# The transfers of the forget-bias rows are issued from the SP queue instead of ScalarE's

## The chip, the cores and the metric

The kernel runs on one core of a Trainium2 chip. The metric is the device time of one execution in microseconds. The core has TensorE (PE in the profile; its weight loads are PEld), VectorE (DVE), ScalarE (ACT), GpSimd (POOL) and SyncE (SP). SP does no arithmetic here: its queue issues transfers. ScalarE has a queue from which it can issue transfers too, between its own instructions.

## The reference

The program computes two layers of a decoder trunk for one sequence of 512 positions and 1024 features in float32. A layer normalises the residual, projects it to queries, keys, values and gates of sixteen heads of 64 features, runs two kinds of attention, gates and projects the result, adds it to the residual, and adds a gated embedding. Eight heads are dilated (three windows mixed) and eight are forgetting heads. For a forgetting head the logit of query i and key k has the difference of two running sums of log forget gates added:

```python
c = jnp.cumsum(log_f.astype(jnp.float32), axis=1).transpose(0, 2, 1)
s = jnp.einsum('bqhd,bkhd->bhqk', q_i, k, preferred_element_type=jnp.float32) * scale
s = s + c_i[..., :, None] - c[:, :, None, :]
```

The part that depends on the query alone drops out of the softmax, so the kernel adds only the row of the key, one row of 512 numbers for each head.

## The kernel before

Float32 products are made on TensorE from pairs: each matrix is split into a high part and a remainder, and a product is three matmuls (`mm3`, over line 88). The weights come from memory by SP (`load`, line 115) into one of three raw buffers, and are split by ScalarE (line 157, `whi`) and VectorE (line 158, `wlo`); the raw buffer is then free for the third load after it. Calls of `W.pump` in the program place these splits among the other work.

In each layer a loop runs over `p`, the eight pairs of heads: pairs 0 to 3 are dilated, 4 to 7 are forgetting. An iteration projects pair `p` for four blocks of 128 positions (`pj`, evacuated by `ev`: squares on ScalarE at line 440, values at line 451, a power on GpSimd at line 445), makes scores and softmax of pair `p-1` (`att_s`: lines 597 to 601), multiplies the probabilities of pair `p-2` with the values (`att_pv`), computes the gate of pair `p` (`gate_mm`, then line 482 on VectorE and line 483 on ScalarE), transposes the probabilities (`att_tp`, evacuated by `att_pt` at lines 621 and 622) and the queries and keys (`att_z`, evacuated by `att_qk` at lines 548 to 556). All matmuls stand on TensorE in the order of the program text. The order on the other engines and in the queues is drawn up ahead of time by a planner, from the text, the dependencies and estimated costs; an engine and a queue then execute their own list strictly in order, each item waiting for what it needs.

At `p == 4` the running sums are made (`cumulate`): a high part by ScalarE into `C2[0:8]` (line 513) and a remainder by VectorE into `C2[32:40]` (line 514). `bias_rows(p)` then copies, for the two heads of pair `p`, one row of high parts and one of remainders from `C2` into four partitions of `CB`: four transfers of 2 KB. It is called at `p` = 4, 5, 6 and 7 of both layers, so there are 8 groups and 32 transfers. They are issued from ScalarE's queue (line 523). A group needs `C2`, and its target `CB` must have been read by the scores of the pair before. It is read by the scores of its own pair one iteration later: the matmuls `psS<-CB,tri` and `psM<-CB,tri` in `att_s`, with 64 rows of `CB` for a head, of which all but two are zero.

Of the kernel before, what the change touches and what calls it, by code (L numbers as in the profile page):

```python
# [9 lines left out]
F32 = mybir.dt.float32  # L10
# [191 lines left out]
def trunk(tc, ap):  # L202
    nc = tc.nc
    V, A, G, T = nc.vector, nc.scalar, nc.gpsimd, InOrder(tc, nc.tensor)
    ctx = ExitStack()
    with ctx:
# [63 lines left out]
        CB = cp.tile([P, S], F32R, name="CB")  # L270
# [247 lines left out]
        def bias_rows(a):  # L518

            for j in range(2):  # L520
                h = 2 * (a - NDIL) + j
                for i in range(2):
                    A.dma_start(CB[64 * j + i:64 * j + i + 1].bitcast(F32),  # L523
                                C2[32 * i + h:32 * i + h + 1].bitcast(F32))


# [157 lines left out]
        for l in range(DEPTH):  # L684
# [58 lines left out]
            for p in range(1, NPAIR):  # L743
# [30 lines left out]
                if NDIL <= p < NPAIR and a >= NDIL:  # L774
                    bias_rows(p)
                pj(p, 3)
                ev(p, 3)
                if p == NDIL:
                    cumulate()
                    bias_rows(p)  # L780
# [186 lines left out]
```

## Time and profile before

| what | value |
|---|---|
| median of the runs | 712.31 us |
| the profiled execution, device time | 712.22 us |
| its span (first to last instruction) | 710.4 us |
| TensorE busy with matmuls | 699.4 us (98%) |
| TensorE loading weights | 618.4 us (87%) |
| VectorE busy | 501.8 us (71%) |
| ScalarE busy | 382.3 us (54%) |
| GpSimd busy | 182.9 us (26%) |
| mean granted TensorE clock | 0.999 |

Busy times leave out what a queue does: the issue of a transfer by ScalarE is in no busy time, but shows as a row of ACTq, ScalarE's queue. So ScalarE can be held up while it counts as idle. The 1.8 us between the span and the device time lie around the first and the last instruction.

### The profile page before, as it was taken

The numbers are of one execution on the slowest core, as the hardware profiler recorded it, in microseconds if no ns is written. First come the engines' busy times: TensorE is split into PE (matmuls) and PEld (weight loads), VectorE is DVE, ScalarE is ACT, GpSimd is POOL, SyncE is SP. The second block draws the span as 40 slices with busy tenths as digits, with TensorE's granted clock in tenths as the row PEclk, the third lists the DMA queues.
The fourth block names the chain that finished last, engine by engine and source line by source line (L and its number), as shares of the span: only waits on it lengthen the run. The fifth ranks groups of instructions, "written<-read, shape, count | busy, mean of one in ns | idle before, by whom it ended". The sixth has DMA issues, their size and how long they took to land.

```text
span 710.4 us, 12211 instructions
## 1 busy us (share of the span) xinstructions
PE 699.4 (98%) x4424; PEld 618.4 (87%) x4424; DVE 501.8 (71%) x1240; ACT 382.3 (54%) x809; POOL 182.9 (26%) x326
## 2 busy tenths in 40 slices
PE   9999999999999999999999999999999999999997
PEld 8999898989989878888899899998889897888886
DVE  7887787766767677838738687777767767694633
ACT  8575556555555756525425556555654656582310
POOL 7462643313131320000004533614131240200000
PEclk9999999999999999999999999999999999999999
DMA  8612131221212145424423022222222113353211
GB/s 289 194 32 68 57 99 50 86 68 54 90 57 88 36 139 150 157 83 156 139 69 119 8 90 60 84 67 70 73 65 86 60 61 119 105 163 118 89 44 45
DMA packets 23948, 65.53 MB, mean 92 GB/s; under 512 B 4817, under 2 KB 6097, under 8 KB 23889
## 3 DMA queue, kind: packets, MB, share of 16 engines
q1 hardware_dynamic: 22576, 64.68, 28.6%
q8 instruction: 35, 0.57, 0.3%
q10 hardware_dynamic: 1312, 0.08, 0.1%
q14 instruction: 25, 0.20, 0.1%
HBM read 60.49 MB, written 4.19 MB: 91 GB/s over the span
## 4 chain that ended last, share of the span: by engine, by line
PE 64%; DVE 17%; ACT 8%; issue 4%; POOL 4%; ACTq 2%; DMA 0%; POOLq 0%; DVEq 0%
PE psA L88 42%; PE psS L88 16%; DVE wlo L158 5%; PE psM L88 4%; POOL f L445 3%; DVE PT L622 3%; ACT U L599 3%; ACTq L523 2%; ACT PT L621 1%; DVE U L597 1%; DVE U L653 1%; ACT whi L157 1%; ACT sqh L483 1%; DVE V L452 1%; DVE ms L442 1%
## 5 line engine op out<-in xcount | busy, mean ns | idle before, releaser
L157 ACT ACTIVATE whi<-raw 128x1024 fp32r<-128x1024 f32 (+3 forms) x105 | 106.7, 1021 | 68.2 <-PE psA L88 51.7
L158 DVE TENSOR_TENSOR wlo<-raw,whi 128x1024 fp32r<-128x1024 f32 (+3 forms) x105 | 122.8, 1171 | 13.3 <-ACT whi L157 13.2
L88 PE MATMUL psA<-whi,X 128*128 128x384 f32 (+1 forms) x480 | 130.5, 341 | 0.0
L88 PE MATMUL psA<-whi,Y 128*128 128x384 f32 (+1 forms) x480 | 129.3, 341 | 0.2 <-DVE U L482 0.2
L445 POOL TENSOR_TENSOR f<-ms,mhalf 128x4 f32<-128x4 f32 x64 | 64.7, 1012 | 243.7 <-DVE ms L443 234.1
L88 PE MATMUL psA<-Y,whi 128*128 128x512 f32 (+1 forms) x320 | 96.6, 385 | 0.7 <-DVE sqh L863 0.5
L88 PE MATMUL psA<-X,whi 128*128 128x512 f32 x304 | 95.7, 396 | 0.0
L599 ACT ACTIVATE U<-U,mx 128x512 f32<-128x512 f32 (+3 forms) x128 | 70.6, 553 | 39.4 <-DVE mx L597 34.5
L88 PEld LDWEIGHTS psA<-whi,X 128*128 128x128 f32 x480 | 87.9, 188 | 1.8 <-ACT whi L157 0.5
L88 PEld LDWEIGHTS psA<-whi,Y 128*128 128x128 f32 x480 | 87.5, 188 | 1.4 <-issue 0.4
L88 PE MATMUL psA<-wlo,X 128*128 128x384 f32 (+1 forms) x240 | 81.8, 341 | 1.7 <-DVE wlo L158 1.7
L88 PE MATMUL psA<-wlo,Y 128*128 128x384 f32 (+1 forms) x240 | 81.3, 339 | 1.2 <-DVE wlo L158 1.2
L601 POOL TENSOR_SCALAR U<-U,sm 128x512 f32<-128x512 f32 (+3 forms) x128 | 65.8, 534 | 55.0 <-DVE sm L600 54.2
L88 PEld LDWEIGHTS psA<-Y,whi 128*128 128x128 f32 x320 | 58.4, 188 | 13.5 <-DVE sqh L863 1.2
L88 PEld LDWEIGHTS psA<-X,whi 128*128 128x128 f32 x304 | 56.5, 188 | 13.1 <-DVE sqh L863 0.4
L88 PE MATMUL psA<-Y,wlo 128*128 128x512 f32 (+1 forms) x160 | 61.3, 383 | 0.0
L88 PE MATMUL psA<-X,wlo 128*128 128x512 f32 x152 | 59.9, 394 | 0.0
L458 DVE TENSOR_TENSOR z<-psA,f 128x256 f32<-128x256 f32 x60 | 25.4, 423 | 45.9 <-POOL f L445 45.9
L622 DVE TENSOR_TENSOR PT<-psS,PT 128x512 fp32r<-128x512 f32 (+1 forms) x58 | 37.1, 673 | 19.1 <-ACT PT L621 19.1
L440 ACT ACTIVATE sq<-psA 128x256 f32<-128x256 f32 x56 | 21.3, 381 | 53.4 <-PE psA L88 45.8
L88 PEld LDWEIGHTS psA<-wlo,X 128*128 128x128 f32 x240 | 45.2, 188 | 3.2 <-DVE wlo L158 3.2
L88 PEld LDWEIGHTS psA<-wlo,Y 128*128 128x128 f32 x240 | 45.1, 188 | 2.0 <-DVE wlo L158 2.0
(190 smaller groups left out, 1232.5 us busy)
## 6 DMA issues: line engine op xcount, KB each, us to landing
raw<-in_wq_dram SPq DMA_DIRECT2D x28, 576.0 KB, 3.9
raw<-in_wg_dram SPq DMA_DIRECT2D x16, 512.0 KB, 3.4
raw<-in_wo_dram SPq DMA_DIRECT2D x16, 512.0 KB, 3.4
raw<-in_wpg_dram SPq DMA_DIRECT2D x16, 512.0 KB, 3.4
raw<-in_wq_dram SPq DMA_DIRECT2D x14, 384.0 KB, 3.3
U<-in_xT_dram SPq DMA_DIRECT2D x16, 256.0 KB, 3.9
raw<-in_wple_dram SPq DMA_DIRECT2D x4, 512.0 KB, 3.6
hs<-U SPq DMA_DIRECT2D x8, 256.0 KB, 3.2
```

Of the source, the lines that this page charges most:

```text
L88: return self.tc.keep_in_program_order(self.eng.matmul(*a, **k))
L157: self.nc.scalar.activation(hi, r, AF.Copy)
L158: eng.tensor_tensor(lo, r, hi.bitcast(F32), op=ALU.subtract)
L440: A.activation(sq, ps[:, :2 * P].rearrange("p (h d) -> p h d", h=4), AF.Square)
L442: V.tensor_reduce(ms, sq, axis=AX.X, op=ALU.add)
L445: G.tensor_tensor(f, ms, mhalf.to_broadcast([P, 4]), op=ALU.pow)
L452: V.scalar_tensor_tensor(v2[:, t, :, HD:P], vps, st["r"][:, t:t + 1], v2[:, t, :, 0:HD].bitcast(F32), op0=ALU.mult, op1=ALU.subtract)
L458: last["V"] = V.tensor_tensor(z, ps[:, :2 * P].rearrange("p (h d) -> p h d", h=4), f[:, :, None].to_broadcast([P, 4, HD]), op=ALU.mult)
L523: A.dma_start(CB[64 * j + i:64 * j + i + 1].bitcast(F32), C2[32 * i + h:32 * i + h + 1].bitcast(F32))
L599: A.activation(seg, seg, AF.Exp, bias=mx, scale=-1.0, accum_out=sm)
L601: G.tensor_scalar(seg, seg, sm, 1.0, op0=ALU.mult, op1=ALU.mult)
L622: last["V"] = V.tensor_tensor(lo, src, hi.bitcast(F32), op=ALU.subtract)
```

## The change

The four transfers of `bias_rows` are issued through `nc.sync`, the SP queue, on which the loads of the weights and the reads and writes of the residual stand. Source, target, size, number, and place in the program text stay as they are.

```diff
@@ -520,7 +520,7 @@
             for j in range(2):
                 h = 2 * (a - NDIL) + j
                 for i in range(2):
-                    A.dma_start(CB[64 * j + i:64 * j + i + 1].bitcast(F32),
+                    nc.sync.dma_start(CB[64 * j + i:64 * j + i + 1].bitcast(F32),
                                 C2[32 * i + h:32 * i + h + 1].bitcast(F32))
```

## Rows read from the trace of the kernel before

**Rows 1.** The page, section 1: busy time, share of the span, instructions.
```profile
PE 699.4 (98%) x4424; PEld 618.4 (87%) x4424; DVE 501.8 (71%) x1240; ACT 382.3 (54%) x809; POOL 182.9 (26%) x326
```
**Rows 2.** Busy time in three stretches: limits, length, then PE, PEld, DVE, ACT, POOL, clock.
```profile
140.00:256.00 116.00, 114.22 (x817) 101.89 (x817) 83.58 (x213) 66.50 (x154) 28.75 (x46) 1.00 0.24 74
256.00:488.00 232.00, 231.82 (x1380) 204.29 (x1379) 164.57 (x388) 121.51 (x243) 53.88 (x90) 1.00 0.31 98
488.00:605.00 117.00, 115.44 (x832) 103.45 (x830) 84.92 (x220) 67.32 (x157) 29.28 (x47) 1.00 0.24 75
```
**Rows 3.** The page, section 4: shares of the chain that ended last, by engine.
```profile
PE 64%; DVE 17%; ACT 8%; issue 4%; POOL 4%; ACTq 2%; DMA 0%; POOLq 0%; DVEq 0%
```
**Rows 4.** The tile CB: its transfers (ns min/median/max, starts), and their time to landing.
```profile
L523 ACTq DMA_DIRECT2D CB<-C x32: 504/546/1271, 147.4 to 585.5; - x32
...
DMA to landing us min/median/max: 1.6/1.7/4.5
```
**Rows 5.** Timeline of ACT, first group: start, us, what [idle before, what ended it].
```profile
147.44 2.52 ACTq L523 DMA_DIRECT2D CB<-C  x4
150.01 0.63 ACT L483 ACTIVATE sqh<-U 128x512 f32<-128x512 f32 x1 [2.60 <-issue]
```
**Rows 6.** Timeline of DVE behind the first group.
```profile
148.16 0.69 DVE L482 TENSOR_TENSOR U<-psA,Rh 128x512 f32<-128x512 f32 x1
151.30 1.29 DVE L622 TENSOR_TENSOR PT<-psS,PT 128x512 fp32r<-128x512 f32 x2 [2.45 <-ACT PT L621]
...
154.00 0.95 DVE L158 TENSOR_TENSOR wlo<-raw,whi 128x768 fp32r<-128x768 f32 x1
```
**Rows 7.** Timeline of PE at the stall behind the first group, and at undisturbed pace.
```profile
154.09 0.33 PE L88 MATMUL psA<-whi,X 128*128 128x384 f32 x1
155.00 0.44 PE L88 MATMUL psA<-wlo,X 128*128 128x384 f32 x1 [0.58 <-DVE wlo L158]
...
186.22 0.51 PE L88 MATMUL psA<-whi,X 128*128 128x384 f32 x2
```
**Rows 8.** Timeline of ACT, the end of the second group and what follows.
```profile
175.13 0.60 ACTq L523 DMA_DIRECT2D CB<-C  x1
175.83 0.39 ACT L440 ACTIVATE sq<-psA 128x256 f32<-128x256 f32 x1 [0.98 <-ACT U L599]
...
180.59 0.63 ACT L483 ACTIVATE sqh<-U 128x512 f32<-128x512 f32 x1 [3.06 <-DVE U L482]
```
**Rows 9.** Timeline of DVE behind the second group.
```profile
178.61 1.35 DVE L158 TENSOR_TENSOR wlo<-raw,whi 128x1152 fp32r<-128x1152 f32 x1
179.88 0.68 DVE L482 TENSOR_TENSOR U<-psA,Rh 128x512 f32<-128x512 f32 x1
```
**Rows 10.** Waits of PE for the split of weights: us in total, times, longest.
```profile
PE psA L88 <- DVE wlo L158: 2.9, 8, 0.6
```
**Rows 11.** Timeline of PE: four more stalls, the first two with no group near.
```profile
5.88 0.70 PE L88 MATMUL psA<-wlo,X 128*128 128x392 f32 x1 [0.20 <-DVE wlo L158]
...
123.64 0.45 PE L88 MATMUL psA<-wlo,X 128*128 128x384 f32 x1 [0.37 <-DVE wlo L158]
...
185.94 0.44 PE L88 MATMUL psA<-wlo,X 128*128 128x384 f32 x1 [0.39 <-DVE wlo L158]
...
529.85 0.41 PE L88 MATMUL psA<-whi,Y 128*128 128x384 f32 x1 [0.18 <-DVE U L482]
```
**Rows 12.** Waits of the SP queue: us in total, times, longest.
```profile
SPq L115 <- DVE wlo L158: 543.0, 90, 21.8
```
**Rows 13.** Timeline of SP: two loads behind the first group.
```profile
161.48 0.33 SPq L115 DMA_DIRECT2D raw<-in_wq_dram  x1
166.52 0.33 SPq L115 DMA_DIRECT2D raw<-in_wg_dram  x1
```
**Rows 14.** Timeline of PE: the first matmuls that read the first group's rows.
```profile
166.56 0.40 PE L88 MATMUL psS<-CB,tri 64*128 64x512 f32 x2
```
**Rows 15.** The page, section 6: loads, KB each, median us from issue to landing.
```profile
raw<-in_wq_dram SPq DMA_DIRECT2D x28, 576.0 KB, 3.9
```

## The prediction

> **What bounds the kernel now.** I read the page's busy times first, then the same times by stretch, then the chain, and only then the place of the change. TensorE is busy 98% of the span [rows 1]. By stretch [rows 2] it idles 116.00 − 114.22 = 1.78 us in 140 to 256 and 117.00 − 115.44 = 1.56 us in 488 to 605, the two stretches that hold the 8 groups and what follows them, but only 0.18 us in the 232 us between, at a granted clock of 1.00 in all. So the matmuls set the time, and the change can touch TensorE's idle time alone: 3.34 us where the groups stand.
>
> The chain seems to say more: 2% of it is ACTq, ScalarE's queue [rows 3], some 14 us of 710. That is a share of one path through the other engines. TensorE worked beside it nearly all the time, and those parts of the path can shrink without moving the end.
>
> **What is removed.** ScalarE loses 32 issues of 546 ns (median; 504 to 1271) [rows 4], 17.5 us of its queue. In the first group of a layer the four stand between ScalarE's instructions: it issues from 147.44 for 2.52 us, and its next instruction, the gate's tanh, starts at 150.01 after 2.60 us of idleness that nothing but the issue explains [rows 5]. Its input was ready when VectorE ended line 482, at 148.16 + 0.69 = 148.85 [rows 6]. So the tanh, and all behind it, can come 150.01 − 148.85 = 1.16 us earlier, not 2.6. Behind it the trace runs: evacuation of the transposed probabilities on ScalarE, its remainder on VectorE at 151.30 after 2.45 us of waiting for ScalarE, and at 154.00 the split of the weights for the matmul at hand [rows 6]. For that split TensorE waits: a matmul starts at 155.00, 0.91 us after the one before it [rows 7], where two such matmuls take 0.51 us together and one 0.34, hence 0.17 apart [rows 7]. The stall costs 0.74 us: 0.58 idle and 0.16 by which the earlier one's shadow covers it. A relief of 1.16 us removes it whole.
>
> In the second group the first issues run under the exponentials and cost nothing. The last two stand out: the last is issued at 175.13, and the next instruction starts at 175.83 after 0.98 us of idleness [rows 8]. The idleness is put down to ACT itself, which had long been done, so I put it down to the issues. What follows goes squares, power on GpSimd, scaling, split of weights, and line 482 right behind that split on VectorE [rows 9]; the tanh waited 3.06 us for it [rows 8]. Each link starts as the one before it ends, so the relief of 0.98 us carries to the split for which TensorE stalls by 0.39 us [rows 11], and 0.39 + 0.16 = 0.55 is less than 0.98.
>
> **The sum.** TensorE waited 2.9 us in 8 stalls for such a split [rows 10]. Two of them have no group near, 0.20 and 0.37 [rows 11], which leaves 2.33 us in 6 stalls, behind the first three groups of each layer. One more wait of 0.18 us, for line 482, stands behind a group [rows 11]. That is 2.51 us of idleness, and with 0.16 us for each of 7 stalls, 1.12, a gain of 3.63 us. The last group of a layer stands before further small stalls: 3.34 − 2.51 = 0.83 us of the idle time is there or scattered. They hang on the values' matmuls after the loop, where ScalarE and VectorE have several evacuations in a row; I count them at nothing. With them, and 0.16 for each of about four, 1.5 us, the largest gain would be 5.1 us. The lower bound of the gain is nothing, if other waits take the stalls' place: the stall of 0.37 us at 123.64 shows that one of this kind forms with no issue on ScalarE.
>
> **What is added to SP.** 32 issues. SP's own take 0.33 us [rows 13], ScalarE's 0.55; so 1.3 to 2.2 us for a group. SP waits for splits 543 of 710 us [rows 12], so the time is there. Two waits come with it. The rows wait for `C2` and for the last reading of `CB`; the loads behind them wait too. For the first group `C2` is complete only at about 148.1, so a load listed behind it would go out up to about 4 us late. Such a load fills a buffer that is read three splits on, and splits, to judge by the loads that they let out, are 5 us apart [rows 13]: some 10 us of slack, no cost. Other loads are further from the groups. The rows in turn may wait behind loads. They land 1.7 us after their issue [rows 4], by 4 × 0.55 + 1.7 = 3.9 us as a group, some 151, and the first reading is at 166.56 [rows 14]. That slack of 15 us is the cover; the price once it is gone is a rival below. In bytes nothing changes: 2 KB each.
>
> Against the profiled execution's 712.22 us the sum gives 712.2 − 3.6 = **708.6 us**. The median of the runs is 712.31, 0.1 away, so both name the same start.
>
> **Rivals.**
>
> *The waits are only handed on.* The planner draws up ScalarE's and VectorE's lists anew without the issues, and may put the splits elsewhere; or the relief ends at VectorE, busy 72% in these stretches. For it: the stall at 123.64. Against it: each chain above is unbroken, and the relief is longer than the stalls. At no gain the time is 712.3; if each of the 8 groups got a stall like 123.64's, 0.37 + 0.16 = 0.53, in addition, 716.5.
>
> *The rows come late.* SP executes in order and stands 76% of the time waiting for a split [rows 12]. If the planner lists a group behind loads whose splits come much later, the scores wait for `CB` on TensorE, in program order with everything behind them. For the first group it takes the load at 166.52: then the rows go out from 166.85 for 1.3 us and land 1.7 us later, at 169.9, against the reading at 166.56: 3.3 us. Listed behind the load at 161.48 they land at about 164.8, in time. With eight such groups 26.6 us, and 712.2 − 3.6 + 26.6 = 735. It passes 2% (14.2 us) from six groups on: 17.8 us, which is 14.2 + 3.6. Against it: a group is ready 10 us or more before that load, and a planner that takes what is ready would not pass it over.
> A rule makes this a little worse: the Trainium skill, "DMA: Bandwidth & Descriptors", section on queues, rings and completion order, has SP and ScalarE own one ring each on the same 16 engines, worked off in ring order. A load lands after 3.9 us [rows 15]; rows right behind that at 161.48 would by the rule land only after it, at 165.4 or later, close to 166.56. No row here shows small transfers behind a load on one queue; the slack of the likeliest order, 15 us, covers 3.9.
>
> *The chain's share comes back whole.* 2% of 710 is 14 us: 698. That would need TensorE to have room at its pace. The Trainium skill, "Perfetto Trace Analysis", section on the most-contended engine, says just this, that matmul busy time is no measure of headroom and the weight loads' share is; that share is 87% here, which would leave 13% of room. The trace speaks against it for this change: PEld is busy 88% of the stretch without groups (204.29 of 232.00), 88% of the two with them (101.89 of 116.00, 103.45 of 117.00) [rows 2]. If the issues slowed TensorE beyond its idle time, the share would drop there.
>
> **How the numbers follow.** Stalls gone, 707.1 to 710: 0.62. Handed on, with no gain or with new stalls, 711 to 716.5: 0.31, most of it within 2 us of 712.3. Rows late: 0.04, half of it past 2%. The whole share: 0.02; a remainder of 0.01 for a faster one still. The predicted time is the first case's. The range reaches from 706.0, a little beyond the largest gain (707.1), to 714.5, which takes in the second case but for its end: about 0.88, and less than that since the bounds are estimates. A difference of under 2% (14 us, what a measurement of this kernel can tell from no change) has 0.95: the first case and nearly all of the second lie in it. Faster by more: 0.02, the third rival. Slower by more: 0.03, late rows in six or more groups, or a worse list.
>
> **What would show it.** Right: no L523 on ACTq; the tanh that started 2.57 us after the first issue [rows 5] starts within a few tenths of the end of line 482; the six stalls on line 158 shrink to under 1 us in all; TensorE's idle time in the two stretches falls from 3.34 to about 0.8; SP issues `CB` right after the last reading of the group before. Wrong: TensorE waiting at `psS<-CB,tri` for a DMA (late rows); loads that land after ScalarE asks for them; stalls on line 158 as long as before, at other places (handed on). A gain of over 5.1 us would say that the idle time is not the bound that I take it for.

## The result, and the profile after

The changed kernel takes 706.61 us (four runs, 706.42 to 706.83). Of the four runs of the kernel before, one took 1372.89 us and is left out here; the other three have a median of 711.92 (712.12 with it). So the change takes off 5.3 us, a ratio of 0.9925 with a 95% interval of 0.9906 to 0.9945. The forecast was 708.6 and the range 706.0 to 714.5; the sign and the mechanism were right, the size was too small. The difference is clear of the noise and under the 2% to which the prediction gave 0.95.

From the page of the changed kernel, section 1, and section 4's shares by engine, which answer to [rows 1, 3]:

```profile
PE 696.0 (99%) x4424; PEld 618.3 (88%) x4424; DVE 502.3 (71%) x1240; ACT 382.3 (54%) x809; POOL 183.5 (26%) x326
...
PE 88%; DVE 6%; ACT 3%; POOL 1%; issue 1%; DMA 0%; ACTq 0%; POOLq 0%; DVEq 0%
```

ScalarE's queue is gone from the chain, and TensorE's share of it rose from 64% to 88%: nearly everything on the way to the end is now a matmul. The same three stretches as in [rows 2] (limits, length, then PE, PEld, DVE, ACT, POOL, clock):

```profile
140.00:256.00 116.00, 115.75 (x838) 104.62 (x837) 86.48 (x227) 68.73 (x162) 30.05 (x49) 1.00 0.25 76
256.00:488.00 232.00, 231.82 (x1374) 204.50 (x1373) 163.98 (x393) 122.43 (x250) 55.72 (x94) 1.00 0.31 97
488.00:605.00 117.00, 116.75 (x843) 105.17 (x843) 86.63 (x226) 68.29 (x159) 30.42 (x49) 1.00 0.24 75
```

TensorE's idle time fell from 1.78 to 0.25 us and from 1.56 to 0.25, further than the forecast, some 0.8 for both together. The stretch between, without groups, kept its 0.18. The tile CB [rows 4] and the waits of PE [rows 10]:

```profile
L523 SPq DMA_DIRECT2D CB<-C x32: 497/580/1242, 147.3 to 575.7; - x32
...
DMA to landing us min/median/max: 1.6/1.8/3.8
```

```profile
PE psA L88 <- DVE wlo L158: 1.2, 4, 0.4
```

The first group, on SP, ACT, DVE and PE, against [rows 5 to 7]:

```profile
147.31 3.16 SPq L523 DMA_DIRECT2D CB<-C  x4
...
148.71 0.63 ACT L483 ACTIVATE sqh<-U 128x512 f32<-128x512 f32 x1 [1.47 <-DVE U L482]
...
147.98 0.69 DVE L482 TENSOR_TENSOR U<-psA,Rh 128x512 f32<-128x512 f32 x1
150.00 1.29 DVE L622 TENSOR_TENSOR PT<-psS,PT 128x512 fp32r<-128x512 f32 x2 [1.32 <-ACT PT L621]
152.58 0.69 DVE L484 SCALAR_TENSOR_TENSOR U<-sqh,U 128x512 f32<-128x512 f32 x1
153.18 0.95 DVE L158 TENSOR_TENSOR wlo<-raw,whi 128x768 fp32r<-128x768 f32 x1
...
154.19 0.44 PE L88 MATMUL psA<-wlo,X 128*128 128x384 f32 x1 [0.25 <-DVE wlo L158]
```

The tanh of line 483 starts right when line 482 ends (148.67), as forecast, and no longer behind four issues. But VectorE now does line 484 ahead of the split of the weights, which it did not do there before, so 0.25 us of the stall stays.

The second group, on ACT, DVE and PE, against [rows 8, 9, 11]:

```profile
173.72 0.36 ACT L440 ACTIVATE sq<-psA 128x256 f32<-128x256 f32 x1
178.52 0.63 ACT L483 ACTIVATE sqh<-U 128x512 f32<-128x512 f32 x1 [3.12 <-DVE U L482]
...
176.48 1.35 DVE L158 TENSOR_TENSOR wlo<-raw,whi 128x1152 fp32r<-128x1152 f32 x1
177.80 0.69 DVE L482 TENSOR_TENSOR U<-psA,Rh 128x512 f32<-128x512 f32 x1
...
184.27 0.34 PE L88 MATMUL psA<-whi,X 128*128 128x384 f32 x1
184.44 0.34 PE L88 MATMUL psA<-wlo,X 128*128 128x384 f32 x1
```

The squares follow without a gap, all of the chain comes earlier, and the two matmuls are 0.17 us apart. Of the waits on SP (us in total, times, longest):

```profile
SPq L115 <- DVE wlo L158: 503.4, 90, 21.8
...
SPq L523 <- PE psM L88: 11.0, 6, 2.0
```

The rows wait up to 2.0 us for the last reading of CB, and no load is late for it: the loads on both sides of the second group go out at 165.49 and 177.86, the rows from 167.83 to 170.2, and ScalarE waits for no load in the two stretches with groups.

The matmuls are the same 4424 in the same order, so their starts can be compared one by one. Between the last starts lie 6.1 us; 6.0 of them are at the groups. (The span of the profiled executions lost 5.7, since the end behind the last matmul was 0.46 us longer, which no step accounts for.)

| matmuls behind the group of | forecast, us | measured, layer 1 / layer 2 |
|---|---|---|
| p = 4 | 0.74 each | 0.62 / 0.63 |
| p = 5 | 0.55 / 0.86 | 0.81 / 1.04 |
| p = 6 | 0.37 / 0.39 | 0.47 / 0.50 |
| p = 7 | 0 | 1.37 / 0.56 |

### The profile page after: what moved, and what is told of

The parts are those of the page before. It is cut to its first block, busy times and chain, and to the rows that moved or that the text cites. A ratio compares the mean times of both kernels' runs of the same rounds, so it can differ in the third digit from the quotient of the medians.

```text
span 704.7 us, 12212 instructions
## 1 busy us (share of the span) xinstructions
PE 696.0 (99%) x4424; PEld 618.3 (88%) x4424; DVE 502.3 (71%) x1240; ACT 382.3 (54%) x809; POOL 183.5 (26%) x326
## 4 chain that ended last, share of the span: by engine, by line
PE 88%; DVE 6%; ACT 3%; POOL 1%; issue 1%; DMA 0%; ACTq 0%; POOLq 0%; DVEq 0%
PE psA L88 60%; PE psS L88 20%; PE psM L88 5%; PE psS L91 2%; DVE PT L622 2%; DVE wlo L158 1%; PE psM L91 1%; PE psA L91 1%; ACT U L599 1%; POOL f L445 1%; ACT PT L621 1%; DMA gn<-in_gn_dram 0%; DVE U L482 0%; ACT sqh L483 0%; DVE U L484 0%
## 5 line engine op out<-in xcount | busy, mean ns | idle before, releaser
L406 POOL TENSOR_TENSOR r<-m,mhalf 128x4 f32<-128x4 f32 x4 | 4.7, 1186 | 162.0 <-DVE m L405 162.0
```

The costliest lines, as they stand in the source:

```text
L406: G.tensor_tensor(r, m, mhalf.to_broadcast([P, NT]), op=ALU.pow)
```

## The experiments

**The theory**: ScalarE stands in a chain that ends at a stall of TensorE; an issue there that doesn't run under another of its instructions delays the chain, by as much of it as the next instruction would not have waited for anyway. What takes the issues over matters only if it is in such a chain itself. **Rivals**: SP helps (its ring, or rows that go out earlier); the planner's new lists, VectorE's above all, make the gain; the mere number of issues on ScalarE counts. Four kernels were compared with 712.5 us for the kernel before.

**act_idle**: the issues stay on ScalarE and move behind a split, for p = 5 to 7.

```diff
...
-                if NDIL <= p < NPAIR and a >= NDIL:
-                    bias_rows(p)
...
+                if p > NDIL:
+                    with tc.issue_after(W.last_hi.ins): bias_rows(p)
```

> ScalarE still issues all 32 row transfers, but for p = 5, 6, 7 of each layer the four stand behind the split of the next weights and ahead of the gate's tanh, a place where ScalarE waited 3.06 us for VectorE's line 482. Theory (ScalarE's time where it is short): six of the eight groups cost nothing any more, and the time between matmul starts that the change took off behind them, 4.6 us, goes here too: 707 to 708.5 us against some 712.1 before and 706.6 after. Rival (SP itself is what helps: its ring, or rows that go out earlier): the rows go out some 3 us later than before and from ScalarE's queue, so no gain: 711.5 to 712.5. Rival (what counts is the number of issues on ScalarE): 712.

Measured: 707.65 us, ratio 0.9933 (0.9921 to 0.9946). Its timeline of ACT at the second group:

```profile
174.31 0.50 ACTq L523 DMA_DIRECT2D CB<-C  x1
...
174.85 0.60 ACTq L523 DMA_DIRECT2D CB<-C  x1
174.90 0.36 ACT L440 ACTIVATE sq<-psA 128x256 f32<-128x256 f32 x1
175.17 0.36 ACT L451 ACTIVATE V<-psA,r 128x128 fp32r<-128x128 f32 x1
175.42 1.16 ACT L157 ACTIVATE whi<-raw 128x1152 fp32r<-128x1152 f32 x1
175.49 1.24 ACTq L523 DMA_DIRECT2D CB<-C  x2
179.64 0.63 ACT L483 ACTIVATE sqh<-U 128x512 f32<-128x512 f32 x1 [3.06 <-DVE U L482]
```

Six groups cost nothing though ScalarE issues all 32 (by the starts of the matmuls behind them they gave 4.7 us, as much as in the changed kernel): the four run under its own instructions and its wait for line 482. SP's list is that of the kernel before. So neither SP nor the number of issues is what counts: their place is.

**act_two**: ScalarE issues two transfers of two rows in place of four.

```diff
-                for i in range(2):
-                    A.dma_start(CB[64 * j + i:64 * j + i + 1].bitcast(F32),
-                                C2[32 * i + h:32 * i + h + 1].bitcast(F32))
+                A.dma_start(CB[64 * j:64 * j + 2].bitcast(F32),
+                            C2[h:h + 33:32].bitcast(F32))
```

> ScalarE issues the rows as before, but two transfers of two rows each in place of four of one row: half the issues. Theory: behind the exponentials only the last issue can still stand out, some 0.2 us of the 0.98, less than the slack, so nearly all of the 4.6 comes back there; in the first groups some 1.2 of the 2.5 us of issue is gone, which is the 1.16 us that could be of use: together 707 to 709 us. Rival (the queue matters, not the issue time): 712.

Measured: 707.42 us, 0.9929 (0.9916 to 0.9941). An issue of two rows took 0.48 us (median), no more than one of one row. In the second group the last one runs under an exponential, and the squares follow at once:

```profile
173.78 0.48 ACTq L522 DMA_DIRECT2D CB<-C  x1
...
174.44 0.19 ACT L599 ACTIVATION_READ_ACCUMULATOR U<-U,mx 128x1 f32 x1
174.53 0.36 ACT L440 ACTIVATE sq<-psA 128x256 f32<-128x256 f32 x1
```

Half the issues give back nearly all. Behind the first groups, where some 1.2 us was expected back, the stalls stayed (0.79 and 0.59 us idle): a transfer of two rows waits for the remainder of line 514 too, so the issues begin at 147.93 and not at 147.44, one of them took 1.06 us, and VectorE does line 484 ahead of the split there, as in the changed kernel.

**first_only, rest_only**: SP for the first group of a layer alone (the edit below), and for the other three alone (with the two engines swapped).

```diff
-                    nc.sync.dma_start(CB[64 * j + i:64 * j + i + 1].bitcast(F32),
+                    (nc.sync if a == NDIL else A).dma_start(CB[64 * j + i:64 * j + i + 1].bitcast(F32),
```

> Only the first group of each layer (p = 4) is issued by SP, the other six by ScalarE. Theory: the first groups' part alone, 0.6 us a layer in the matmul starts, so 710.9 us (710.4 to 711.4). Rival (the gain comes from lists that the planner draws anew all over): anything between 706.6 and 712, without the stalls behind the other groups staying as they were.

> The counterpart: p = 5, 6, 7 of each layer on SP, the first group on ScalarE. Theory: 712.1 less 4.6, 707.5 us (707 to 708.2), and the two parts add up to the whole 5.5. Rival (the parts lean on each other, through loads and lists): the sum of the parts misses the whole by over 1 us.

Measured: 709.99 us, 0.9966 (0.9953 to 0.9978), and 708.07 us, 0.9939 (0.9926 to 0.9953). The second is near its forecast; the first gained 2.5 us, twice what was expected, and the sum, 6.9, is 0.9 to 1.6 more than the whole (5.3, and 6.1 in the comparison below). By the matmul starts at the groups the excess is 1.2 us, and the trace of first_only shows where it lies. The stalls behind the second groups shrank too, by 0.27 and 0.54 us in the matmul starts, to 0.26 and 0.24 us idle from 0.39 and 0.36, though the issues were still there and ScalarE still idled 0.98 us behind them. A delay of the first group was carried on into the next iteration by VectorE and by the power on GpSimd that it waits for: line 442, at 162.81 before, comes at 162.31, 0.50 us earlier, while the matmuls there start only 0.24 us earlier. So two terms of my sum, the first and the second group's, removed in part the same wait. Another 0.4 us of first_only may be chance: one issue at the fourth group took 0.88 us in place of 1.27, and the wait for line 482 behind it is gone.

**act_extra, sp_extra**: four more transfers in each group, which copy zero rows onto zero rows, on ScalarE (the edit below) or on SP (`nc.sync` in its place); "C" is the instruction of line 513. Beside these, the next kernel and the changed kernel, the kernel before took 712.75 us.

```diff
...
+                    with behind("C"):
+                        A.dma_start(CB[64 * j + i + 2:64 * j + i + 3].bitcast(F32),
+                                        CB[64 * j + i + 4:64 * j + i + 5].bitcast(F32))
```

> The rows go by SP as in the changed kernel; beside that ScalarE again issues four transfers of 2 KB in each group, which copy zero rows of CB onto other zero rows of CB, at the places in its list where the real ones stood before. Theory (ScalarE's time): the stalls behind the groups come back, 711 to 713 us. Rivals (what helps is that the rows are issued by SP, on its ring, or at an earlier time): 706 to 707.5 us, since all that is kept.

> The same zero-row transfers, issued by SP: twice the issues on SP, 64 in place of 32. Those of the first group of a layer may be listed earlier among the loads. Theory (SP has the time: it waits for splits most of the span, and loads go out well ahead of their use): 706 to 707.3 us, no new stall. Rival (the loads behind the rows are near their limit on SP): 2 to 3 us more issue in each of eight groups shows as waits for raw on ScalarE and stalls on line 158: 709 us or more.

> The changed kernel itself, for the comparison on the same chip: 706.6 us against 712.1 for the kernel before.

Measured: act_extra 711.25 us, 0.9981 (0.9972 to 0.9990); sp_extra 706.36 us, 0.9915 (0.9902 to 0.9929); the changed kernel 706.67 us, 0.9920 (0.9906 to 0.9933). In act_extra, ACT and PE at the second group:

```profile
174.95 0.55 ACTq L526 DMA_DIRECT2D CB<-CB  x1
175.59 0.38 ACT L440 ACTIVATE sq<-psA 128x256 f32<-128x256 f32 x1 [1.04 <-issue]
...
185.69 0.44 PE L88 MATMUL psA<-wlo,X 128*128 128x384 f32 x1 [0.40 <-DVE wlo L158]
```

The idleness and the stall of [rows 8, 11] are back while the rows themselves go by SP. 4.6 of some 6 us returned. The rest stayed off mainly behind the first groups (0.10 and 0.06 us idle there): these four issues do not wait for `C2`, so the tanh starts 0.52 us behind the end of line 482, in place of 1.16, and VectorE's list is not quite that of before (both queries' remainders ahead of the second line 622). On SP, twice the issues cost nothing.

**gate_last**: the changed kernel, with line 484 put behind the split on VectorE. **before_edge**: the same edge in the kernel before.

```diff
-        eng.tensor_tensor(lo, r, hi.bitcast(F32), op=ALU.subtract)
+        self.last_lo = eng.tensor_tensor(lo, r, hi.bitcast(F32), op=ALU.subtract)
...
-                with behind("V"):
+                with behind("V"), tc.issue_after(W.last_lo.ins):
                     rest()
```

> The changed kernel with one more edge for the planner: the product that ends the gate (line 484, needed only an iteration later) stands behind the split of the weights on VectorE. In the changed kernel it stood ahead of that split where TensorE still stalled, by 0.25 us behind the first group of each layer and 0.37 us at 123.45. Theory (what is left behind the first groups is VectorE's order, 0.6 us of line 484, and no longer ScalarE): the three stalls go, 0.53 + 0.40 + 0.42 = 1.35 us by the spacing of the matmul starts, so 1.35 us below the changed kernel: about 705.3 us. Rival (ScalarE's chain is what is late there, or the values' matmuls then wait for VectorE): within 0.4 us of the changed kernel.

> The kernel before (rows issued by ScalarE) with the edge of gate_last, line 484 behind the split of the weights on VectorE. Theory: in the kernel before VectorE had that order behind the groups already; only the stall at 123.6 us, which has the other order, goes: 0.53 us, 711.5 to 712 us. The issues still delay ScalarE, so the other stalls stay. Rival (VectorE's order, and not ScalarE's issues, makes the stalls): 707 us or less.

Measured: gate_last 705.41 us (704.87 to 705.79, the changed kernel beside it 706.28 to 707.05), 0.9902 (0.9888 to 0.9915) of the kernel before. It beats both kernels. Its two stretches and the matmul behind the first group:

```profile
140.00:256.00 116.00, 116.00 (x839) 104.93 (x838) 87.02 (x229) 69.17 (x163) 30.53 (x49) 1.00 0.24 76
488.00:605.00 117.00, 117.00 (x870) 105.86 (x868) 86.18 (x224) 68.08 (x160) 29.87 (x47) 1.00 0.24 75
```

```profile
153.20 0.41 PE L88 MATMUL psA<-wlo,X 128*128 128x384 f32 x1
```

TensorE has no idle time there any more. before_edge took 710.44 us against 712.72, 0.9972 (0.9961 to 0.9982): 2.3 us less, where 0.5 was expected. The expectation had the order wrong: only behind the first groups did VectorE have the split ahead of line 484; behind the second and third it had line 484 first, and there the edge took the stalls away with the issues still on ScalarE. Behind the first groups and the last ones they stayed (0.57, 0.58 and 0.25 to 0.38 us idle). So a stall of 0.4 us has two cures here, 1 us of ScalarE or 0.6 us of VectorE; neither alone does all. For these stalls VectorE's order, the rival, is a cause as good as the issues; for those of the first and last groups it is not.

**pool**: the rows issued by GpSimd (`G.dma_start`).

> The rows are issued by GpSimd's queue. ScalarE's and VectorE's lists are those of the changed kernel. Theory (what helps is that ScalarE is freed, whichever queue takes the issues, if that queue has the time): GpSimd has the scalings of the exponentials and the power of line 445 there, with 1.62 us of idleness ahead of the last power. Four issues there at 0.05 us each cost nothing, 706.6 us; at 1 us each two of them stand out by up to 1 us, in six groups, of which some becomes stalls: up to 709 us. Rival (SP's queue is what helps): 712 us.

Measured: 712.49 us against 712.72, 0.9999 (0.9990 to 1.0008). ScalarE's, VectorE's and TensorE's lists are those of the changed kernel, and the whole gain is gone. POOL and DVE at the second group, then POOL in the changed kernel:

```profile
175.55 1.02 POOL L523 DMA_DIRECT2D CB<-C  x2
176.58 1.04 POOL L445 TENSOR_TENSOR f<-ms,mhalf 128x4 f32<-128x4 f32 x1
...
177.66 0.42 DVE L458 TENSOR_TENSOR z<-psA,f 128x256 f32<-128x256 f32 x1 [2.72 <-POOL f L445]
178.00 1.35 DVE L158 TENSOR_TENSOR wlo<-raw,whi 128x1152 fp32r<-128x1152 f32 x1
```

```profile
175.08 1.02 POOL L445 TENSOR_TENSOR f<-ms,mhalf 128x4 f32<-128x4 f32 x1 [0.57 <-DVE ms L443]
```

With the scalings 1.1 us later for the two issues among them, the power comes 1.5 us later than in the changed kernel, and the split with it; the stalls behind the groups are 0.40 and 0.37 us again. The same lists and another loaded link give the same time as before: the rival of the lists falls, and so does freeing ScalarE as such. The time is the one forecast for the rival that SP's queue is what helps, but act_idle and act_two came to 707.7 and 707.4 us with no row on SP; the theory's price, 709 us at most, was too low.

**rows_late**: the rows by SP, each group right ahead of the scores that read it and behind the last load.

```diff
...
+                if a >= NDIL:
+                    with tc.issue_after(W.last_dma.ins): bias_rows(a)
                 att_s(a)
-                if NDIL <= p < NPAIR and a >= NDIL:
-                    bias_rows(p)
...
```

> The rows go by SP, but each group is issued as late as the program allows, right ahead of the scores that read it, behind the last load that the text has before them. For the first group that is the load at some 165.5 us, just before the reading at 165.8. Theory (the slack is the cover; once it is gone TensorE waits for the rows in its own order): four issues of 0.56 us and 1.8 us to landing make the rows some 3.9 us late in six groups and 2 to 4 us in the last group of each layer, 27 to 31 us in all: 733 to 738 us. Rival (the late rows find other work on TensorE to hide under): under 720 us.

Measured: 748.66 us, 1.0502 (1.0487 to 1.0516). Waits of PE, and two stretches around the second such wait (the columns as above; the eighth number is the granted clock):

```profile
PE psS L88 <- DMA CB<-C: 25.6, 8, 4.6
```

```profile
206.00:210.00 4.00, 3.86 (x26) 3.77 (x26) 1.94 (x7) 1.38 (x3) 0.69 (x1) 0.50 0.02 4
214.00:218.00 4.00, 4.00 (x21) 3.51 (x21) 0.99 (x5) 1.89 (x5) 1.85 (x4) 1.00 0.00 0
```

TensorE waited 25.6 us for the rows, a little under what was expected. But the time rose by 42 against the changed kernel. With each of the six waits of 3.2 to 4.6 us the granted clock fell to 0.50, the 1.2 GHz level, for some us; with the two waits of 1.6 us it stayed at 1.00. TensorE's busy time rose from 696.0 to 713.3 us, and 25.6 + 17.3 = 42.9. By the matmul starts the six waits cost 38.0 us for 22.5 us of waiting, the two short ones 2.2 us each.

## Why the prediction was right, and where its size was off

**What bounds it: right, but idle time is not all of it.** The gain is TensorE's lost time at the groups, and with gate_last that stretch is full. The prediction let the change touch TensorE's idle time alone, 3.34 us, and took a gain of over 5.1 us for a sign that this is not the bound. The sign came. Idle time in the two stretches fell by 2.84 us, and the time that the profile counts as busy fell too, from 699.4 to 696.0 us: a stalled matmul is counted longer (in [rows 7] 0.44 us at 155.00, where the one before it has 0.33). What TensorE loses is read from the matmul starts, not from its idle time. The chain's 2% for ScalarE's queue, 14 us, did not come back; PEld's share rose with the idle time gone, to 90% (104.62 of 116.00), so the room that the share of weight loads seemed to leave was not there for this change.

**The mechanism: right.** act_idle, act_two and act_extra move the stall with the place of the issue on ScalarE, at whichever queue the rows are; pool moves it to another link of the same chain.

**The size: the sum gave 3.6 us, 5.3 to 6.1 were measured.** The step that failed is the one that counted the last groups at nothing: they gave 1.37 and 0.56 us, 1.9 in all. Some 0.7 us of the 1.37 goes back to one issue in the profiled execution, at 235.8, that took 1.27 us in place of some 0.55. The chain of waits had no break from their issues to those stalls either, and it should have been followed there. Their matmuls wait for evacuations of ScalarE and VectorE in a row, and the row starts with the delayed tanh. Second, a stall also delays the matmul after it by 0.10 us, which the 0.16 did not hold; and behind the first groups the values' matmuls had waits of 0.07 to 0.14 us, 0.3 in each layer, that show as no idleness and that I had not seen. Against that, the first groups gave 0.62 rather than 0.74 each, since the planner put line 484 ahead of the split once the tanh came earlier; that is the "handed on" rival in small, in two places. The largest gain that I allowed, 5.1 us, was too low for the same two reasons.

**SP: right on the cover, low on the price.** An issue of a row takes SP 0.58 us, a little over my upper end of 0.55. The slack of 15 us holds, as sp_extra shows.

**The late rows: right as a mechanism, its price too low.** The rival had 3.3 us for a group, 735 us for eight. The wait was 3.2 us on average; what was missing is the clock that falls with it, and some 0.6 us for each wait beyond its length, as the two short ones show. The rule of the Trainium skill ("DMA: Bandwidth & Descriptors", section on queues, rings and completion order) that a ring is worked off in order agrees with rows_late: there the rows took 2.6 us to land (median; 1.8 in the changed kernel), and in all eight groups the first row landed 0.16 to 0.20 us after the load of 512 KB ahead of it on SP's queue (in the first group 169.40 against 169.21). That the ring is the reason is not shown: in the kernel before, the row that ScalarE's queue issued at 496.30 landed as closely behind a load of SP's queue, 499.07 against 498.90.

**Open.** The end behind the last matmul, 0.46 us longer (so too when the changed kernel was run again and in gate_last, but not in sp_extra).

## What to carry to other kernels

The issue of a transfer is an instruction of the engine that issues it: look at what stands behind it in that engine's list, follow the waits from there to the engine that bounds the kernel, and put the issue on a queue that no such chain passes, or in a place where its engine waits anyway. Rows of the same kind can share an issue. The gain is what the bounding engine loses, not the time of the issues (17.5 us here for 5.3 to 6.1), and two delays in one chain are not to be added up.

## What the runs showed that was not expected

- An issue of one row of 2 KB takes 0.55 us on ScalarE, 0.58 on SP and 0.53 on GpSimd (medians), one of two rows 0.48, while a load of 512 KB took SP 0.33.
- In every profile but that of pool, one or two issues of a row took 0.8 to 1.9 us, on either queue, and nearly all of them at about 149, 199 or 235 to 240 us of the span (1.27 at 235.8 before, 1.24 at 149.2 after, 1.39 at 234.8 in act_idle). What stretches them was not tried.
- ScalarE's queue issues ahead of the engine: in act_idle the issues are listed behind the split, which starts at 175.42, and the second of them starts at 174.85. So the issues next to running instructions are free, and only what is left when the engine has run dry stands out.
- The six waits of over 3 us in rows_late, 22.5 us, cost 38.0 us by the matmul starts, the two of 1.6 us 2.2 each. If 0.6 us of every wait is put down to the wait itself, as with the short ones, some 12 us is an estimate of what the lower clock cost.
